# Issue-order edges between projection tiles and the state-mixing groups of a hybrid decoder block

## The chip, the cores and the metric

The kernel runs on one core of a Trainium2 chip. The metric is the device time of one execution in microseconds (us). The kernel before takes 984.88 us, the median of three runs (984.75 to 986.89). Engines are named as in the profile: PE is TensorE (matmuls, PEld its weight loads), DVE is VectorE, ACT is ScalarE, POOL is GpSimd, SP is SyncE, which issues most loads; ACTq and POOLq are the DMA issues of ACT and POOL.

## What is computed

One layer of a decoder block on 512 tokens of width 1024, all in float32. A projection of the normalised input feeds three things: r, k, v and low-rank ("lora") inputs of an RWKV-7 state recurrence over 12 heads, q, k, v of a dilated attention over 12 heads, and two gates. Cut to what matters here:

```python
h = modulate(rms_norm(x, g_pre_mix[i]), shift_m, scale_m)      # shift, scale: adaLN columns from c
p = h @ w_in[i]
pr, pk, pv, pw, pa, pg = _split(p_shift, ...)                  # token-shifted
wf = w0 + jnp.tanh(pw) @ w2                                    # lora: decay
a = jax.nn.sigmoid(a0 + pa @ a2)                               # lora: in-context rate
def step(state, inp):                                          # RWKV-7, one token
    sa = -jnp.einsum('bhvk,bhk->bhv', state, kk_t)
    state = state * w_t + sa[..., None] * (kk_t * a_t) + v_t[..., None] * k_t
    return state, jnp.einsum('bhvk,bhk->bhv', state, r_t)
y_a = (group_norm(y) + bonus) * gate @ w_a
y_b = dilated_attention_mix(pq, pk_att, pv_att, w_b)           # 3 groups of 4 heads
x = x + gate_m * rms_norm((sigmoid(ga) * y_a + sigmoid(gb) * y_b) @ w_out)
x = x + gate_f * rms_norm(swiglu(modulate(rms_norm(x))))
```

## The kernel before

**Tiles.** Every float32 matmul is done as three matmuls on split operands (`split`: `hi` a cast on ACT, L111, `lo` a subtraction on DVE, L112; `mm3`). One tile of the input projection takes 128 output columns: its 512 KB of weights are loaded, split (one `hi`, one `lo` of 128x1024), and `gemm_in` runs 8 steps of 3 matmuls of 128x512, 24 in all, into one PSUM bank. What follows depends on the kind. In the strings of `SEQ` each tile has a letter and a number: `r`, `k`, `v` are RWKV tiles (`rkv_tile`, a scale on ACT and a shift on DVE, L208), `G` gates, `Q` and `K` attention tiles (`spill_qk`: four DVE operations of rotary embedding, L227 to L236, and a store to DRAM), `V` attention values, `W` tiles of the output projection of the RWKV part. `A1` is one column of the adaLN table (a DVE multiply with accumulation, 128x1024, L168, on weights that SP loads), `N` a norm of the keys.

**Groups.** The RWKV heads are done in two groups of six heads, three pairs each (`rwkv_group(0)`, `rwkv_group(1)`; here the first and second group). For each pair PE does the lora matmuls (`lw`, `la` with `uw`, `ua`), from which ACT and DVE make decays; DVE forms `AR` and `BK` (L468 to L476); PE does the gram matmuls of AR and BK (L481, in `mm` L108), DVE masks them into `Sg` (L486), ACT copies blocks of them to `xg` (L490). PE also transposes BK (L496), computes the bonus and transposes v (L509). When all three pairs are there, DVE transposes `xg` to `fU` (L518) and inverts the triangular 32x32 blocks by 31 steps of small products and sums (L526, L530), then transposes the result to `T1` (L534). PE multiplies with it (`t1`, L547 on), and eight chunks of the recurrence follow, each a chain over PE, ACT and DVE. At the end of a group the result is normalised, transposed back (L639) and stored per pair as `d_z` (L646).

**Attention.** It reads q, k and v back from DRAM (L703 to L706) after a cosine/constant load into `cs` (L696), takes scores on PE, row maxima, exponentials on ACT (L762, L765), transposes, sums and the product with v; two of its results and the `z` of the RWKV part feed the `W` tiles.

**What sets the order.** The program is written tile by tile: `run(SEQ[0])`, group 0, `run(SEQ[1])`, group 1, `run(SEQ[2])`, attention, `run(SEQ[3])`. A scheduler places the instructions on the engines by its own estimate of when each is ready; `tc.high_priority(PRI)` around the groups and the attention lets their pieces go ahead of tiles that stand before them in the text. The result is one fixed instruction list per engine; every engine works its list in order and waits where an operand is not there.

Of the kernel before, what the change touches and what calls it, by code (L numbers as in the profile page):

```python
# [81 lines left out]


@with_exitstack
def block_kernel(ctx, tc, x, vec, cst, cst2, cst3, crow, ada, win0, lora, wts, wa, out):
# [21 lines left out]
    def mm(o, l, r, start, stop):  # L107
        return nc.tensor.matmul(o, l, r, start=start, stop=stop)  # L108

# [17 lines left out]
    def mm3(o, wh, wl, ah, al, start, stop):  # L127
        mm(o, wh, ah, start, False)
        mm(o, wh, al, False, False)
        mm(o, wl, ah, False, stop)  # L130

# [77 lines left out]

    def gemm_in(i):  # L210
        wh, wl = weights(i)
        ps = bank("mm")
        for k in range(KT):
            w = slice(k * P, (k + 1) * P)
            mm3(ps, wh[:, w], wl[:, w], hh[:, k, :], hl[:, k, :], k == 0, k == KT - 1)
        return ps
# [42 lines left out]

    def filler(i):  # L260
        ps = gemm_in(i)
        flush()
        return ps
# [110 lines left out]
    def rkv_tile(kind, pi):  # L374
        ci = {"r": 0, "k": 6, "v": 12}[kind] + pi
        ps = gemm_in(W_RK + RK_ORDER.index((kind, pi)))
        rkv[kind, pi] = tmp()[:, 0:S]
        shift_evac(ps, ci, rkv[kind, pi])
# [19 lines left out]
    def rwkv_group(gi):  # L398
# [20 lines left out]
        for p in range(GP):  # L419
            pi = p0i + p  # L420
            cols = slice(p * P, (p + 1) * P)
            sgm = rp.tile([P, 2, NCH, 2 * C], F32, tag="Sg", name=nm("Sg"), bufs=3)
            Sg[p] = sgm
            scr.append(sgm.rearrange("p e c t -> p (e c t)"))

            ps = bank(BT[gi][1])
# [8 lines left out]
            mm(ps, ua[hi64, cols], lw_l[hi64], False, True)  # L435
            A.activation(scr[p][:, 1040:1552], ps, AF.Sigmoid, bias=vcol(V_A0, pi))
        for p in range(GP):
            pi = p0i + p
# [38 lines left out]

            sgm = Sg[p]
            for c0 in (0, 4):
                pgr = [bank(BT[gi][6]), bank(BT[gi][7])]  # L480
                for c in range(c0, c0 + 4):  # L481
                    for e in range(2):
                        rows = slice(64 * e, 64 * e + 64)
                        mm(pgr[e][:, (c - c0) * P:(c - c0 + 1) * P], bk[rows, c, :], ar[rows, c, :], True, True)
                for e in range(2):
                    V.tensor_tensor(out=sgm[:, e, c0:c0 + 4, :], in0=pgr[e].rearrange("p (c t) -> p c t", c=4),  # L486
                                    in1=m_gram[:, None, :].to_broadcast([P, 4, 2 * C]), op=ALU.mult)
            for e in range(2):
                for b in range(2):
# [9 lines left out]
        for p in range(GP):  # L499
# [148 lines left out]
    def gate_tile(i):  # L648
        ps = filler(W_GATE + i)
        g = tmp("tg", 3)[:, 0:S]  # L650
# [4 lines left out]
    def run(seq):  # L655
        for item in seq.split():
# [9 lines left out]
            elif kind == "V":  # L666
                spill_v(filler(W_ATT + (n // 2) * 6 + 4 + n % 2), n // 2, d_v[n // 2][n % 2])
            elif kind == "Q":
                spill_qk(filler(W_ATT + (n // 2) * 6 + n % 2), n // 2, n % 2, d_q[n // 2][n % 2])
            elif kind == "K":  # L670
                spill_qk(filler(W_ATT + (n // 2) * 6 + 2 + n % 2), n // 2, n % 2, d_k[n // 2][n % 2])
# [387 lines left out]
```

## Time and profile before

| | before |
|---|---|
| median of three runs | 984.88 us |
| the profiled execution's own time | 985.46 us |
| its span (first to last instruction) | 983.4 us |
| PE busy | 943.3 us |
| DVE busy | 578.5 us |
| ACT busy | 394.2 us |
| POOL busy | 43.9 us |
| mean granted clock of PE | 0.982 |

The span holds all instructions; the time has 2.1 us around it. PE's busy time includes stretches at half the clock, in which the same matmuls take about twice as long, so its share of the span doesn't tell how close PE is to its best. PE's idle time and the granted clock are what an order of work can change. The other engines have time to spare over the whole span, but not in every stretch.

### The profile page before, as it was taken

What the parts mean: (1) busy time and instruction counts of PE and PEld (TensorE: products, weight loads), DVE (VectorE), ACT (ScalarE), POOL (GpSimd) and SP (SyncE); (2) the same over time, 40 slices, a digit from 0 to 9 for tenths busy, and PEclk for the clock granted to TensorE, in tenths of its full rate; (3) what the DMA queues carried; (4) which work ended last, traced back from release to release, by engine and by line L of the source; (5) the groups of instructions that cost most, each with busy time, mean ns of one, the idle gap of its engine ahead of it and who ended that gap; (6) DMA issues with size and microseconds to landing.
All of it is one profiled execution on the core that took longest, in us unless ns stands there. A gap on an engine that the chain in (4) does not pass through costs nothing.

```text
span 983.4 us, 13640 instructions
## 1 busy us (share of the span) xinstructions
PE 943.3 (96%) x5372; PEld 755.8 (77%) x5372; DVE 578.5 (59%) x1050; ACT 394.2 (40%) x631; POOL 43.9 (4%) x89
## 2 busy tenths in 40 slices
PE   6999999899989999997999899999999999999997
PEld 4886878677677776786887678988888888888885
DVE  7985789764799956685555677573333333322234
ACT  7567562433466333321472246532323222221223
POOL 0000000100100010020000100010000000000000
PEclk9998999999989999999899999999999999999999
DMA  9753215543221334249336862163242323233322
GB/s 376 276 172 102 87 54 170 174 152 106 89 70 61 110 118 150 87 166 281 99 104 226 277 224 80 44 235 107 86 129 87 107 88 105 89 104 92 101 86 85
DMA packets 47169, 131.71 MB, mean 134 GB/s; under 512 B 11249, under 2 KB 12033, under 8 KB 47106
## 3 DMA queue, kind: packets, MB, share of 16 engines
q1 hardware_dynamic: 27792, 96.74, 30.3%
q10 hardware_dynamic: 13970, 16.27, 5.3%
q0 software_dynamic: 5344, 17.84, 4.8%
q8 instruction: 42, 0.69, 0.3%
q14 instruction: 21, 0.17, 0.1%
HBM read 116.14 MB, written 14.69 MB: 133 GB/s over the span
## 4 chain that ended last, share of the span: by engine, by line
PE 71%; DVE 12%; issue 8%; DMA 4%; ACT 3%; ACTq 1%; POOL 0%; SPq 0%; DVEq 0%; POOLq 0%
PE ps L108 69%; DVE lo L112 2%; DVE fP L526 2%; DVE fT L530 2%; DMA d_ya<-t 1%; DMA k<-d_k 1%; ACT xg L490 1%; DMA x<-in_x_dram 1%; DMA gb<-d_gate 1%; ACT hi L111 1%; PE ps L308 1%; PE ps L496 0%; DVE T L534 0%; PE ps L917 0%; DMA aw<-in_ada_dram 0%
## 5 line engine op out<-in xcount | busy, mean ns | idle before, releaser
L111 ACT CAST hi<-raw 128x1024 fp32r<-128x1024 f32 (+1 forms) x130 | 132.9, 1024 | 363.2 <-PE ps L108 309.9
L112 DVE TENSOR_TENSOR lo<-raw,hi 128x1024 fp32r<-128x1024 f32 (+1 forms) x130 | 154.6, 1189 | 169.3 <-ACT hi L111 167.0
L108 PE MATMUL ps<-hl,hi 128*128 128x512 f32 x432 | 175.4, 406 | 0.0
L108 PE MATMUL ps<-hh,lo 128*128 128x512 f32 x432 | 174.7, 404 | 0.0
L108 PE MATMUL ps<-hh,hi 128*128 128x512 f32 x432 | 173.6, 411 | 0.5 <-ACT hi L111 0.5
L108 PE MATMUL ps<-h2h,hi 128*128 128x512 f32 (+1 forms) x352 | 133.6, 381 | 0.7 <-ACT u L947 0.7
L108 PE MATMUL ps<-h2l,hi 128*128 128x512 f32 (+1 forms) x352 | 133.6, 381 | 0.0
L108 PE MATMUL ps<-h2h,lo 128*128 128x512 f32 (+1 forms) x352 | 133.4, 380 | 0.0
L108 PEld LDWEIGHTS ps<-hh,hi 128*128 128x128 f32 x432 | 83.1, 193 | 19.4 <-issue 1.1
L108 PEld LDWEIGHTS ps<-hh,lo 128*128 128x128 f32 x432 | 82.9, 192 | 17.9 <-issue 0.7
L108 PEld LDWEIGHTS ps<-hl,hi 128*128 128x128 f32 x432 | 83.3, 193 | 16.6 <-issue 0.2
L108 PEld LDWEIGHTS ps<-h2h,hi 128*128 128x128 f32 x352 | 66.0, 188 | 13.5 <-ACT u L947 0.9
L108 PEld LDWEIGHTS ps<-h2l,hi 128*128 128x128 f32 x352 | 66.1, 188 | 12.8
L108 PEld LDWEIGHTS ps<-h2h,lo 128*128 128x128 f32 x352 | 66.1, 188 | 12.5
L168 DVE SCALAR_TENSOR_TENSOR aw<-aw,silur 128x1024 f32<-128x1024 f32 x48 | 58.3, 1218 | 5.8 <-DMA aw<-in_ada_dram 5.7
L948 DVE TENSOR_TENSOR u<-u,ps 128x512 f32<-128x512 f32 x22 | 15.0, 687 | 66.3 <-PE ps L108 58.7
L108 PE MATMUL ps<-lo,fh 128*128 128x512 f32 x144 | 44.4, 389 | 0.0
L108 PE MATMUL ps<-hi,fl 128*128 128x512 f32 x144 | 44.4, 389 | 0.0
L108 PE MATMUL ps<-hi,fh 128*128 128x512 f32 x144 | 44.3, 390 | 0.0
L108 PEld LDWEIGHTS ps<-lo,fh 128*128 128x128 f32 x144 | 27.0, 188 | 5.6
L108 PEld LDWEIGHTS ps<-hi,fh 128*128 128x128 f32 x144 | 27.0, 188 | 5.6
L108 PEld LDWEIGHTS ps<-hi,fl 128*128 128x128 f32 x144 | 27.0, 188 | 5.6
(294 smaller groups left out, 1365.7 us busy)
## 6 DMA issues: line engine op xcount, KB each, us to landing
raw<-in_wts_dram SPq DMA_DIRECT2D x124, 512.0 KB, 3.6
aw<-in_ada_dram SPq DMA_DIRECT2D x40, 512.0 KB, 4.4
d_gate<-t POOLq DMA_DIRECT2D x16, 256.0 KB, 2.4
aw<-in_ada_dram POOLq DMA_DIRECT2D x8, 512.0 KB, 4.7
raw<-in_win_dram SPq DMA_DIRECT2D x8, 384.0 KB, 6.6
raw<-in_wa_dram SPq DMA_DIRECT2D x8, 384.0 KB, 3.0
x<-in_x_dram SPq DMA_DIRECT2D x4, 512.0 KB, 5.0
t<-d_gate ACTq DMA_DIRECT2D x8, 256.0 KB, 4.0
```

The source lines that it names most:

```text
L108: return nc.tensor.matmul(o, l, r, start=start, stop=stop)
L111: A.copy(hi, src)
L112: V.tensor_tensor(out=lo, in0=src, in1=r32(hi), op=ALU.subtract)
L168: V.scalar_tensor_tensor(out=aw, in0=aw, scalar=1.0, in1=silur, op0=ALU.mult, op1=ALU.mult, accum_out=modv[:, i:i + 1])
L308: nc.tensor.transpose(pt[:, i * P:(i + 1) * P], xt[i][:, j * P:(j + 1) * P], ident)
L490: A.copy(xg[64 * e + 32 * b:64 * e + 32 * b + 32, :, p * NCH:(p + 1) * NCH], sgm[32 * b:32 * b + 32, e, :, 32 * b:32 * b + 32].rearrange(" ...
L526: V.tensor_tensor(out=pv, in0=fU[:, t + 1 + a:t + 1 + b, t, None].to_broadcast([P, b - a, m]), in1=fT[:, t, None, 0:m].to_broadcast([P, b ...
L530: V.tensor_tensor(out=rows, in0=rows, in1=pv, op=ALU.add)
L948: V.tensor_tensor(out=u, in0=u, in1=pg, op=ALU.mult)
```

## The change

Three things are changed; no arithmetic is.

1. `SEQ`: the third part has its attention tiles in another order (Q0, K2, K4, Q1, K1 instead of Q1, K1, K2 and Q0, K4 at the end), and the gate tile G9 moves from the head of the fourth part to the end of the third. The fourth part runs under an issue edge behind the last attention matmul of its kind (`issue_after`).
2. In `rwkv_group` the transposes of v (four for each pair, and two ACT copies to `UV`) move from behind the bonus to a loop of their own right after the lora matmuls.
3. A table `JOINTS` gives six edges. Each ties one recorded set of PE matmuls (the lora matmuls of group 0, the grams of pair 1 and 2 of group 0, the first `t1` matmuls of group 0, the grams of pair 0 of group 1, the first `t1` matmuls of group 1) to a step of a tile (`gemm_in` records the last matmul of each of its 8 steps): the set may not be placed ahead of that step. The edge is one of order alone; no semaphore is waited on for it.

```diff
@@ -77,8 +77,12 @@
-       "V5 V1 V0 V4 V2 K0 V3 Q1 K1 A1 A1 K2 A1 A1 Q3 A1 Q0 A1 Q5 A1 K4",
-       "G9 G10 G11 G12 G15 W0 G14 W1 W4 W2 W3 W5 W6 W7"]
+       "V5 V1 V0 V4 V2 K0 V3 Q0 K2 A1 A1 K4 A1 A1 Q1 A1 K1 A1 Q3 A1 Q5 G9",
+       "G10 G11 G12 G15 W0 G14 W1 W4 W2 W3 W5 W6 W7"]
+
+
+JOINTS = [("lora0", "v2", 5), ("gram01", "G4", 7), ("gram02", "k5", 7), ("inv0", "G8", 3),
+          ("gram10", "V5", 4), ("inv1", "V2", 7)]
...
     def mm(o, l, r, start, stop):
-        return nc.tensor.matmul(o, l, r, start=start, stop=stop)
+        i = nc.tensor.matmul(o, l, r, start=start, stop=stop)
+        if joint[0] is not None:
+            joined.setdefault(joint[0], []).append(i)
+        return i
+
+    joint, joined, steps = [None], {}, {}
...
+    def join():
+        for name, item, k in JOINTS:
+            if name in joined and item in steps:
+                for i in joined.pop(name):
+                    tc.add_manual_dep(ins_of(i), ins_of(steps[item][k]).name,
+                                      mybir.DependencyInfo(mybir.DependencyClass.NoSync, mybir.DependencyReason.DATA), reason="joint")
...
+        for p in range(GP):
+            v = rkv["v", p0i + p]
+
+            pt = bank(BT[gi][5])
+            for t in range(NTT):
+                nc.tensor.transpose(pt[:, t * P:(t + 1) * P], v[:, t * P:(t + 1) * P], ident)
+            ptv = pt.rearrange("p (i e w) -> p i e w", i=NTT, e=2)
+            for par in range(2):
+                A.copy(UV[64:128, par::2, :, p, :], ptv[64 * par:64 * par + 64])
...
-
-            pt = bank(BT[gi][5])
-            for t in range(NTT):
-                nc.tensor.transpose(pt[:, t * P:(t + 1) * P], v[:, t * P:(t + 1) * P], ident)
-            ptv = pt.rearrange("p (i e w) -> p i e w", i=NTT, e=2)
-            for par in range(2):
-                A.copy(UV[64:128, par::2, :, p, :], ptv[64 * par:64 * par + 64])
...
         for p in range(GP):
             pq = bank("c")
+            joint[0] = f"inv{gi}" if p == 0 else None
...
         flush()
+        join()
```

In the printed orders that follow, a number behind a name tells its buffers apart, and a line of "..." stands for rows that repeat the pattern. Line numbers of the changed kernel are larger (L108 becomes L112, L496 and L466 become L529 and L497, L112 becomes L131).

PE, around the gram matmuls of the second group's first pair (`AR`, `BK` the operands; `ps_2480` is the tile r4, `ps_2514` is v5, `ps_3498` is V5). Before:

```order
L466 MATMUL ps_2630<-cs_67,BK_2629 128x128 x4
L108 MATMUL ps_2480<-hh,hi_2476 128x512
L108 MATMUL ps_2480<-hl,hi_2476 128x512
L108 MATMUL ps_2480<-hh,lo_2477 128x512
...
L108 MATMUL ps_2645<-AR_2628,BK_2629 128x128
L108 MATMUL ps_2646<-AR_2628,BK_2629 128x128
...
L496 MATMUL ps_2673<-cs_67,BK_2629 128x128 x4
L496 MATMUL ps_2679<-cs_67,BK_2629 128x128 x4
L466 MATMUL ps_2696<-cs_67,BK_2695 128x128 x4
L108 MATMUL ps_2514<-hh,hi_2510 128x512
```

After:

```order
L529 MATMUL ps_2694<-cs_67,BK_2650 128x128 x4
...
L464 MATMUL ps_2633<-cs_67,t_2539 128x128 x4
...
L112 MATMUL ps_3498<-hh,hi_3494 128x512
L112 MATMUL ps_3498<-hl,hi_3494 128x512
L112 MATMUL ps_3498<-hh,lo_3495 128x512
...
L112 MATMUL ps_2666<-AR_2649,BK_2650 128x128
L112 MATMUL ps_2667<-AR_2649,BK_2650 128x128
...
L529 MATMUL ps_2700<-cs_67,BK_2650 128x128 x4
L497 MATMUL ps_2717<-cs_67,BK_2716 128x128 x4
```

The gram stood behind 18 matmuls of r4; it stands behind the rest of r4, all of v5 and G13 and 15 matmuls of V5 now, and a transpose of BK and those of v (L464) are ahead of it.

DVE, the end of the second group's chain to T (`fP`, `fT` the small products and sums; `lo` a weight split, `aw` an adaLN column, `t` on L247 to L252 the rotary products of a tile). Before:

```order
L526 TENSOR_TENSOR fP_2852<-fU_2850,fT_2851 128x56 x2
L530 TENSOR_TENSOR fT_2851<-fT_2851,fP_2852 128x2x28 x2
L112 TENSOR_TENSOR lo_3692<-raw_3689,hi_3691 128x1024
L526 TENSOR_TENSOR fP_2852<-fU_2850,fT_2851 128x87
L530 TENSOR_TENSOR fT_2851<-fT_2851,fP_2852 128x3x29
L526 TENSOR_TENSOR fP_2852<-fU_2850,fT_2851 128x60
L530 TENSOR_TENSOR fT_2851<-fT_2851,fP_2852 128x2x30
L526 TENSOR_TENSOR fP_2852<-fU_2850,fT_2851 128x31
L530 TENSOR_TENSOR fT_2851<-fT_2851,fP_2852 128x31
L534 STREAM_TRANSPOSE T_465_2974<-fT_2851 32x1024 x2
```

After:

```order
L556 TENSOR_TENSOR fT_2851<-fT_2851,fP_2852 128x3x29
L252 TENSOR_TENSOR t_3730<-t_3730,t_3728 128x512
L552 TENSOR_TENSOR fP_2852<-fU_2850,fT_2851 128x60
L247 STREAM_SHUFFLE t_3807<-ps_3774 128x512
L556 TENSOR_TENSOR fT_2851<-fT_2851,fP_2852 128x2x30
L249 TENSOR_TENSOR t_3809<-ps_3774,cs_143 128x512
L187 SCALAR_TENSOR_TENSOR aw_3942,modv<-aw_3942,silur 128x1024
L552 TENSOR_TENSOR fP_2852<-fU_2850,fT_2851 128x31
L131 TENSOR_TENSOR lo_3907<-raw_3904,hi_3906 128x1024
L556 TENSOR_TENSOR fT_2851<-fT_2851,fP_2852 128x31
L250 TENSOR_TENSOR t_3807<-t_3807,cs_143 128x512
L560 STREAM_TRANSPOSE T_465_2974<-fT_2851 32x1024 x2
```

One weight split stood among these last steps; now splits, an adaLN column and rotary products of two tiles stand between nearly every two of them.

PE, from the last transposes of the second group (`yb`) to the first attention scores (`k`, `q`; `ps_3992` is the tile Q5, `ps_4034` K4, `ps_4535` G10, `ps_4569` G11, `ps_4637` G15). Before:

```order
L639 MATMUL ps_3480<-cs_67,yb_3081 128x128 x4
L108 MATMUL ps_3992<-hl,hi_3988 128x512
...
L108 MATMUL ps_4034<-hh,hi_4030 128x512
...
L108 MATMUL ps_4535<-hh,hi_4531 128x512
...
L108 MATMUL ps_4126<-k_4085,q_4079 128x128
```

After:

```order
L667 MATMUL ps_3480<-cs_67,yb_3081 128x128 x4
L112 MATMUL ps_4569<-hl,hi_4565 128x512
...
L112 MATMUL ps_4603<-hh,hi_4599 128x512
...
L112 MATMUL ps_4637<-hh,hi_4633 128x512
...
L112 MATMUL ps_4160<-k_4119,q_4113 128x128
```

Between them stood 11 matmuls of Q5, K4, G9 and 9 of G10 (68 matmuls); now 11 of G11, G12 and 4 of G15 (39) stand there, and Q5, K4, G9 and G10 are ahead of the transposes.

## Rows read from the trace of the kernel before

**Rows 1.** The page's busy times of the engines, and the view of cores

```profile
PE 943.3 (96%) x5372; PEld 755.8 (77%) x5372; DVE 578.5 (59%) x1050; ACT 394.2 (40%) x631; POOL 43.9 (4%) x89
...
core 0: 983.4 us, clock 0.982
```

**Rows 2.** Waits of PE: us in total, times, longest us

```profile
PE ps L108 <- DVE BK L474: 5.2, 4, 2.9
PE ps L108 <- DVE T L534: 4.0, 3, 2.1
...
PE ps L509 <- ACT BK L497: 2.5, 2, 1.4
```

**Rows 3.** Windows: us, busy by engine (PE, PEld, DVE, ACT, POOL), clock, DMA, GB/s

```profile
91.00:98.00 7.00, 7.00 (x17) 4.71 (x16) 1.01 (x3) 3.73 (x5) 0.00 (x0) 0.53 0.22 77
279.37:285.40 6.03, 6.03 (x44) 5.81 (x45) 5.27 (x7) 3.15 (x6) 0.00 (x0) 0.51 0.39 105
427.30:522.00 94.70, 88.82 (x522) 73.48 (x520) 54.92 (x75) 38.40 (x69) 7.99 (x15) 0.95 0.54 175
487.00:505.00 18.00, 18.00 (x131) 15.71 (x129) 5.88 (x8) 17.83 (x42) 0.00 (x0) 1.00 0.08 24
```

**Rows 4.** Timeline of PE, 272 to 293: start, us, engine, line, op [idle before]

```profile
274.26 0.39 PE L108 MATMUL ps<-hh,hi 128*128 128x512 f32 x1
...
276.08 0.39 PE L108 MATMUL ps<-hh,lo 128*128 128x512 f32 x1
279.37 3.79 PE L108 MATMUL ps<-AR,BK 64*128 64x128 f32 x32 [2.90 <-DVE BK L474]
283.08 1.97 PE L496 MATMUL ps<-cs,BK 128*128 128x128 f32 x8
```

**Rows 5.** Timeline of PE: first lora matmul; second group, pair 2

```profile
76.21 0.49 PE L108 MATMUL ps<-lw_h,uw 128*128 128x512 f32 x1 [0.70 <-DVE uw L112]
...
301.89 2.06 PE L108 MATMUL ps<-AR,BK 64*128 64x128 f32 x32 [0.42 <-DVE BK L474]
...
308.61 0.66 PE L509 MATMUL ps<-cs,t 128*128 128x128 f32 x4 [1.40 <-ACT BK L497]
```

**Rows 6.** Timeline of PE, first use of T in the second group

```profile
339.17 0.28 PE L108 MATMUL ps<-T,Sg 32*32 32x32 f32 x2 [1.73 <-DVE T L534]
...
343.62 0.63 PE L108 MATMUL ps<-hh,lo 128*128 128x512 f32 x1
...
346.18 0.63 PE L108 MATMUL ps<-hh,lo 128*128 128x512 f32 x1
```

**Rows 7.** Groups of DVE, 308 to 338 us: busy us, mean ns, idle before

```profile
L530 DVE TENSOR_TENSOR fT<-fT,fP 128x110 f32<-128x110 f32 (+35 forms) x59 | 12.5, 251 | 0.1
L526 DVE TENSOR_TENSOR fP<-fU,fT 128x110 f32<-128x110 f32 (+35 forms) x59 | 12.5, 251 | 0.6
L112 DVE TENSOR_TENSOR lo<-raw,hi 128x1024 fp32r<-128x1024 f32 x4 | 4.9, 1219 | 0.0
```

**Rows 8.** Groups of DVE over the whole span, same columns

```profile
L168 DVE SCALAR_TENSOR_TENSOR aw<-aw,silur 128x1024 f32<-128x1024 f32 x48 | 58.3, 1218 | 5.8 <-DMA aw<-in_ada_dram 5.7
...
L230 DVE TENSOR_TENSOR t<-t,cs 128x512 f32<-128x512 f32 x12 | 8.2, 684 | 0.0
```

**Rows 9.** Timelines of PE, POOL and ACT, 426 to 522 us

```profile
427.26 0.60 PE L639 MATMUL ps<-cs,yb 128*128 128x128 f32 x4
430.24 0.54 POOL L646 DMA_DIRECT2D d_z<-bonus  x1 [1.38 <-DVE bonus L645]
438.98 0.33 ACTq L696 DMA_DIRECT2D cs<-in_cst_dram  x1
445.27 2.98 PE L108 MATMUL ps<-k,q 64*128 64x128 f32 x16 [1.94 <-DMA k<-d_k]
460.52 3.63 PE L108 MATMUL ps<-k,q 64*128 64x128 f32 x32 [1.32 <-DMA k<-d_k]
521.92 0.48 PE L108 MATMUL ps<-zh,lo 128*128 128x512 f32 x1
```

**Rows 10.** The page's DMA issues: KB each, median us to landing

```profile
d_gate<-t POOLq DMA_DIRECT2D x16, 256.0 KB, 2.4
```

More of the change, by code (lines that the diff above doesn't have):

```diff
@@ L107, in mm, with ins_of @@
     def mm(o, l, r, start, stop):
-        return nc.tensor.matmul(o, l, r, start=start, stop=stop)
+        i = nc.tensor.matmul(o, l, r, start=start, stop=stop)
[3 more added lines that the diff above has]
+    joint, joined, steps = [None], {}, {}
+    def ins_of(i):
+        return i.ins if hasattr(i, "ins") else i
+    def join():
[4 more added lines that the diff above has]
+                                      mybir.DependencyInfo(mybir.DependencyClass.NoSync, mybir.DependencyReason.DATA), reason="joint")
     def split(hi, lo, src):
@@ L129, in mm3 @@
         mm(o, wh, al, False, False)
-        mm(o, wl, ah, False, stop)
+        return mm(o, wl, ah, False, stop)
     vc = const.tile([P, NV], F32, name="vc")
@@ L208, in shift_evac, with gemm_in @@
         V.scalar_tensor_tensor(out=dst[:, 1:S], in0=ps[:, 0:S - 1], scalar=vcol(V_MU, ci), in1=dst[:, 1:S], op0=ALU.mult, op1=ALU.add)
-    def gemm_in(i):
+    def gemm_in(i, item=None):
         wh, wl = weights(i)
         ps = bank("mm")
+        steps[item] = []
         for k in range(KT):
             w = slice(k * P, (k + 1) * P)
-            mm3(ps, wh[:, w], wl[:, w], hh[:, k, :], hl[:, k, :], k == 0, k == KT - 1)
+            steps[item].append(mm3(ps, wh[:, w], wl[:, w], hh[:, k, :], hl[:, k, :], k == 0, k == KT - 1))
         return ps
@@ L258, in spill_v, with filler @@
         pend.append(rest)
-    def filler(i):
-        ps = gemm_in(i)
+    def filler(i, item):
+        ps = gemm_in(i, item)
         flush()
@@ L375, in rkv_tile @@
         ci = {"r": 0, "k": 6, "v": 12}[kind] + pi
-        ps = gemm_in(W_RK + RK_ORDER.index((kind, pi)))
+        ps = gemm_in(W_RK + RK_ORDER.index((kind, pi)), f"{kind}{pi}")
         rkv[kind, pi] = tmp()[:, 0:S]
@@ L424, in rwkv_group @@
             scr.append(sgm.rearrange("p e c t -> p (e c t)"))
+            joint[0] = f"lora{gi}"
             ps = bank(BT[gi][1])
@@ L435, in rwkv_group @@
             mm(ps, ua[hi64, cols], lw_l[hi64], False, True)
+            joint[0] = None
             A.activation(scr[p][:, 1040:1552], ps, AF.Sigmoid, bias=vcol(V_A0, pi))
+        for p in range(GP):
[6 more added lines that the diff above has]
+                A.copy(UV[64:128, par::2, :, p, :], ptv[64 * par:64 * par + 64])
         for p in range(GP):
@@ L478, in rwkv_group @@
             sgm = Sg[p]
+            joint[0] = f"gram{gi}{p}"
             for c0 in (0, 4):
@@ L487, in rwkv_group @@
                                     in1=m_gram[:, None, :].to_broadcast([P, 4, 2 * C]), op=ALU.mult)
+            joint[0] = None
             for e in range(2):
@@ L547, in rwkv_group @@
                     mm(pq[64 * e + 32:64 * e + 64, c * 32:(c + 1) * 32], Sg[p][0:32, e, c, 32:64], t1a[:, e, :, p * NCH + c], True, True)
+            joint[0] = None
             qs = Qd[:, p % 2]
@@ L648, in gate_tile @@
     def gate_tile(i):
-        ps = filler(W_GATE + i)
+        ps = filler(W_GATE + i, f"G{i}")
         g = tmp("tg", 3)[:, 0:S]
@@ L666, in run @@
             elif kind == "V":
-                spill_v(filler(W_ATT + (n // 2) * 6 + 4 + n % 2), n // 2, d_v[n // 2][n % 2])
+                spill_v(filler(W_ATT + (n // 2) * 6 + 4 + n % 2, item), n // 2, d_v[n // 2][n % 2])
             elif kind == "Q":
-                spill_qk(filler(W_ATT + (n // 2) * 6 + n % 2), n // 2, n % 2, d_q[n // 2][n % 2])
+                spill_qk(filler(W_ATT + (n // 2) * 6 + n % 2, item), n // 2, n % 2, d_q[n // 2][n % 2])
             elif kind == "K":
-                spill_qk(filler(W_ATT + (n // 2) * 6 + 2 + n % 2), n // 2, n % 2, d_k[n // 2][n % 2])
+                spill_qk(filler(W_ATT + (n // 2) * 6 + 2 + n % 2, item), n // 2, n % 2, d_k[n // 2][n % 2])
             elif kind == "A":
```

## The prediction

> **What bounds the kernel now.** The page comes first: TensorE (PE) is busy for 943.3 of 983.4 us, VectorE (DVE) for well under two thirds, so no other engine is the bound over the whole run, and the mean granted clock is 0.982 [rows 1]. Two things are therefore left for a change of order: the 40 us in which PE stands, and the stretches in which it runs at 1.2 instead of 2.4 GHz. A matmul of a projection tile follows the one before after 0.228 us at the full clock (274.26 to 276.08 is eight steps) [rows 4] and after 0.427 us at half (343.62 to 346.18 is six) [rows 6]; a tile of 24 thus costs 5.5 us.
>
> The list of PE's waits comes next. Those that this change can touch are the ones on BK (the last DVE product before a pair's gram matmuls, 5.2 us in four waits), on T (the inverted 32x32 blocks, 4.0 us in three) [rows 2] and on k (the attention's keys coming back from DRAM, 1.94 and 1.32 us) [rows 9]. The timeline around the largest of them shows what such a wait really costs. At 276.3 PE has run out of tiles that the program lets it do and stands 2.90 us until BK is there; the gram matmuls then take 3.79 us [rows 4], where those of another pair take 2.06 [rows 5], and the granted clock from there to 285.4 is 0.51 [rows 3]: it has dropped to half after the idle time. The same is seen behind T: the wait of 1.73 us at 339.17 is followed by matmuls at 0.427 us [rows 6]. So each wait counts with the slow matmuls behind it.
>
> **Part 1: the lora, gram and transposes pieces (edges lora0, gram01, gram02, gram10, and the value transposes).** They remove nothing; they put tiles that PE has anyway ahead of pieces that DVE has not fed yet.
> - lora0: the first lora matmul waits 0.70 us for uw [rows 5]. It now stands six matmuls later (1.4 us at 0.228), which covers it: +0.7 us (gains carry a plus). If the cast of uw is late by as much again, nothing.
> - Pairs 1 and 2 of the first head group: waits on BK there are 5.2 - 2.90 - 0.42 = 1.9 us [rows 2, 4, 5]. The grams of pairs 0, 1 and 2 now stand 18, 14 and 10 tile matmuls later; as pair 0's is later too, DVE starts each pair up to 4.1 us later on PE's account, and pairs 1 and 2 keep less of their shift than it seems. With the transposes of v no longer queued behind a PSUM copy on ScalarE (ACT), which takes up to 2.5 - 1.40 = 1.1 us more [rows 2, 5], I take +1.7 us; bounds 0 and +3.0.
> - The second group: pair 0's gram moves from behind 18 matmuls of r4 to behind 15 of V5, with v5 and G13 in between: from the lora piece on PE has 82 matmuls ahead of it instead of 26, 12.8 us more. What goes is the wait of 2.90, the 0.42 at pair 2, the 1.40 at the bonus and transposes [rows 4, 5], and the slow clock: 3.79 - 2.06 = 1.7 on the gram, and at the same ratio 0.9 of the 1.97 on the transposes. Sum 2.90 + 0.42 + 1.40 + 1.7 + 0.9 = +7.3 us. Late next would be DVE: it was 2.90 behind PE, and the tiles put in between bring it up to four weight splits of 1.22 us [rows 7] and two evacuations, 6.3 us; 12.8 - 2.9 - 6.3 leaves 3.6 us. So it fits, and the bounds are +4.5 and +8.
> - Key norm of the first group: the clock is at 0.53 from 91 to 98 us [rows 3], 3.3 us lost after small matmuls and an idle PE. Value transposes now stand in that neighbourhood and the lora wait ahead of it is gone. Between 0 and +3.3; I take +1.5, the middle, since rows speak for neither end.
>
> The Trainium skill has a rule that speaks against counting the slow clock so high: "TensorE: Matmul & The Clock Gate", Part 1, says that an idle array falls to 1.2 GHz, which the trace shows, and that the ramp costs less than 1% of a typical kernel's span, which would be under 9.8 us here. The trace disagrees: 0.982 of the clock is 1.8%, 17.7 us [rows 1]. By the page's figure the clock parts of my gains (1.7 + 0.9 + 1.5) would shrink to 9.8/17.7 of their size, an estimate of 1.8 us less in the sum; the measurement decides, and my sum goes by it.
>
> **Part 2: the T pieces (edges inv0, inv1).** The first matmul on T waits 2.1 us in the first group, 1.73 in the second [rows 2, 6]. The edges only forbid a place earlier than the third step of G8 and the seventh of V2; the scheduler now puts the pieces at the end of G8 and in K4, later than that. On DVE the chain to T is some 118 small products and sums and a transpose [rows 7], in one in-order queue; what stands in it from other work delays T one for one.
> - First group: 14 more tile matmuls ahead of T (3.2 us), three groups of value transposes (0.66 each [rows 5]) and the 1.1 us of waits less, so PE comes 0.1 us later. DVE has two adaLN columns of 1.22 us more [rows 8] in the chain, and less of splits and evacuations, net about 2.0. The wait grows to about 4: -1.8 us; bounds -4 and +2.
> - Second group: 56 more tile matmuls (12.7 us), minus 2.0 of value transposes and 1.4 of wait, plus 0.5: PE comes 9.8 us later. In the chain now stand seven weight splits instead of four, five adaLN columns instead of none and seven rotary products (tiles K0 and Q0): 3 x 1.22 + 5 x 1.22 + 7 x 0.68 [rows 7, 8] = 14.5, a little less as neighbours overlap: 14.0. The wait becomes 1.73 + 14.0 - 9.8 = 5.9 us. The slow matmuls behind it cost what they cost now. -4.0 us; bounds -6.5 (a later column whose DMA is late) and +1.7 (the wait gone). What is queued behind T on DVE is two more transposes and the recurrence's copies, which wait with it.
>
> **Part 3: the end of the second group and the attention.** Pushing 12 to 13 us of tiles ahead of T, and G9 ahead of the queue, uses up cover. Between the last transposes of the group (427.26) and the last attention matmul (521.92) lie 94.7 us now [rows 9]; in them PE has 211 matmuls of tiles, and in the changed order 100. So 111 x 0.228 = 25.2 us of work stands ahead of that stretch; the stretch has to get shorter by as much, or the difference is lost.
> It can: the cosine load that opens the attention (438.98) waits for the last rotary product of K4 now, 11.7 us after the transposes; after the change it waits for the z of the last pair, whose store is issued at 430.24 [rows 9]; stores from this queue land 2.4 us after issue [rows 10], so about 5.3 us after the transposes. From there 6.3 us to the first scores, the second wait on k, and 61.4 us from 460.52 to the end [rows 9] with 104 tile matmuls of which 49 stay (12.5 us less). What can't shrink is the run of exponentials: ACT is busy 17.83 of 18.00 us from 487 on [rows 3]. If all the 12.5 and the 4.3 us between the two waits go, the stretch is 5.3 + 6.3 + 11.0 + 48.9 = 71.5 us, a loss of 2.0. If half of the 12.5 and none of the 4.3 goes, 82 us, a loss of 12.5. I take -3.0, near the first, since most of the stretch is pieces of attention with tiles between them, which shorten one for one; and leave the other end to a rival.
>
> **The sum.** 0.7 + 1.7 + 7.3 + 1.5 - 1.8 - 4.0 - 3.0 = +2.4 us. Against the profiled execution's own 985.46 that gives 983.1; it lies 0.6 above the median of the three times (984.88), so 982.5 for the median.
>
> **Rivals.**
> - *Slower: the attention runs bare.* With 100 matmuls left, ACT's exponentials leave PE without tiles, it stands, and returns at half clock. For it: 17.83 of 18 us of ACT, two waits on k, a stage whose mean clock is 0.95 [rows 3]. Against it: the first load starts 6 us earlier. The point from which it decides: a stretch from the last transposes to the last attention matmul of more than 74.9 us eats the whole gain; at 82 us the sum is 2.4 - 9.5 = -7.1 us, at 79 us -4.1. Time 989.
> - *No change: T takes it back.* Both T waits at their bounds (-4 and -6.5) cost 4.7 us more: 2.4 - 4.7 = -2.3, with half of that 984.9 to 986. For it: the count of DVE work above is firm, since the queue is in order. Against it: nothing but DMA could make it worse than counted. Time 985.
> - *A larger gain.* The attention loses nothing, and T is there when PE comes: 2.4 + 3.0 + 1.8 + 4.0 = 11.2 at most; with two thirds of it 975. Against it: the DVE count.
> - *The edges do nothing.* The printed order excludes this for gram10 and the lora; for gram01, gram02 and inv1 the pieces stand later than the edge asks, so these edges alone may be idle. This changes who moves the pieces, not the sum.
>
> **How the numbers follow.** A difference within 0.2% (about what a measurement of this kernel can tell from no change) is 982.9 to 986.9. Forecast 0.33 (its own range 979 to 982.9), larger gain 0.10, no change 0.25, slower 0.32. Faster 0.43, same 0.25, slower 0.32. The range for 8 in 10 runs from 974.5, most of the larger gain, to 991, the bare attention at its worse end.
>
> **What would show it.** Right: no wait on BK over 1 us, the gram of the second group's first pair at 2.1 us, and PE's clock at 1.00 around it; T waits of about 4 and 6 us; a stretch of some 72 us from the last transposes to the end of the attention. Wrong: a second-group BK wait that lives on behind V5 (the DVE count in part 1 failed), T waits under 2 us (the count in part 2), or a stretch over 75 us with PE idle beside the exponentials (part 3).

## The result

The changed kernel takes 997.62 us (median of four runs, 996.81 to 1005.31) against 984.82 us of the kernel before on the same chip (983.36 to 986.89): a ratio of 1.0132, 95% interval 1.0089 to 1.0174. It is slower by 12.8 us where 2.4 us less were forecast, and lies outside the range. The rival that comes nearest is the one that it named "the attention runs bare".

The profiled execution takes 996.97 us (span 995.2). The page's busy times and the view of cores of the changed kernel answer to [rows 1]:

```profile
PE 946.8 (95%) x5372; PEld 759.8 (76%) x5372; DVE 578.2 (58%) x1050; ACT 395.2 (40%) x632; POOL 43.8 (4%) x89
...
core 0: 995.2 us, clock 0.972
```

The work is the same; PE is busy 3.5 us longer, since more of it runs at half clock (its mean clock is 0.972 instead of 0.982), and idle 8.3 us longer. Waits of PE in the changed kernel (us in total, times, longest), to be held against [rows 2]:

```profile
PE ps L112 <- DVE T L560: 4.9, 3, 3.2
...
PE ps L112 <- DMA k<-d_k: 3.2, 1, 3.2
PE ps L112 <- DVE BK L505: 3.0, 5, 1.1
PE ps L112 <- ACT zh L130: 2.6, 1, 2.6
PE ps L801 <- ACT S L791: 2.4, 1, 2.4
...
PE ps L801 <- DVE PT L806: 2.2, 1, 2.2
PE ps L112 <- DVE t L249: 2.0, 1, 2.0
```

The waits on BK have gone down from 5.2 to 3.0 us, with none over 1.1; those on T have gone up from 4.0 to 4.9. New, or longer than before, are the waits in the attention (zh, S, PT), and one on `t L249`, a rotary product that holds a PSUM bank.

To see where the time went, one number is worked out from the timelines at six places of every kernel: the start of an event, minus its start in the kernel before, minus 0.2267 us for each tile matmul (`hh`, `hl` against `hi`, `lo`) that PE has done more by then. It is the time lost or gained up to there with the moved work taken out. (The place "after the attention" is the first matmul of the third W tile.) The account is of one profiled execution of each kernel, which can lie far from the kernel's median (e10: 974.76 against 983.98), so a row is evidence only where several kernels show it. The differences from place to place, in us (plus is a loss), against the profiled execution of before:

| stage | predicted | the change |
|---|---|---|
| start to the first T piece (first group) | -3.9 + 1.8 | -2.9 |
| T piece to the second group's lora | 0 | +2.8 |
| lora to the second group's T piece | -7.3 + 4.0 | -2.0 |
| T piece to the last transposes of the group | 0 | +3.7 |
| last transposes to the W tiles after the attention | +3.0 | +12.2 |
| the rest | 0 | -2.0 |
| span | -2.4 | +11.8 |

Most of the miss stands in one row. The stretch from the last transposes to the last attention matmul, PE's timeline of the changed kernel (start, us, engine, line, operation, idle before it and what ended that); beside [rows 9]:

```profile
450.59 0.60 PE L667 MATMUL ps<-cs,yb 128*128 128x128 f32 x4
...
461.83 1.79 PE L112 MATMUL ps<-k,q 64*128 64x128 f32 x16 [1.76 <-DMA VN<-d_v]
...
473.04 4.58 PE L112 MATMUL ps<-k,q 64*128 64x128 f32 x32 [3.23 <-DMA k<-d_k]
480.26 0.50 PE L112 MATMUL ps<-zh,hi 128*128 128x512 f32 x1 [2.65 <-ACT zh L130]
...
499.97 1.94 PE L801 MATMUL ps<-cs,S 128*128 128x128 f32 x7 [2.43 <-ACT S L791]
...
521.65 0.79 PE L801 MATMUL ps<-cs,S 128*128 128x128 f32 x4 [2.17 <-DVE PT L806]
...
532.30 0.48 PE L112 MATMUL ps<-zl,hi 128*128 128x512 f32 x1
```

It is 81.7 us long, 13.0 less than before, with 25.2 us of tile work less in it (96 tile matmuls now stand ahead of it, 15 of the W tiles behind it). Windows of both kernels split its second half at the run of exponentials (us; busy and count of PE, PEld, DVE, ACT, POOL; granted clock; DMA share; GB/s). Before:

```profile
460.50:487.70 27.20, 25.50 (x145) 20.80 (x146) 17.84 (x26) 9.23 (x13) 2.15 (x4) 0.87 0.46 146
487.70:521.90 34.20, 33.26 (x233) 28.81 (x232) 16.90 (x19) 23.91 (x52) 1.62 (x3) 1.00 0.41 133
```

After:

```profile
473.04:499.50 26.46, 21.40 (x128) 16.54 (x128) 16.41 (x24) 5.38 (x8) 1.61 (x3) 0.85 0.49 161
499.50:532.30 32.80, 27.67 (x185) 24.71 (x186) 13.88 (x16) 20.68 (x49) 0.00 (x0) 0.81 0.25 86
```

The second half has 41 tile matmuls instead of 104, 14.3 us of work less, and is 59.3 instead of 61.4 us long. PE's busy time in it has fallen by 9.7 us only, and its idle time has grown from 2.6 to 10.2 us. In the part with the exponentials the clock, 1.00 before, is 0.81, and PE idles 5 us instead of 1. The attention's own matmuls pay for the clock: of four equal sets of 30 one takes 5.2 us and another 4.9, the other two 3.6 and 3.5. The first two of them, after:

```profile
504.96 5.22 PE L112 MATMUL ps<-PT,VN 128*128 128x128 f32 x30
...
512.68 3.62 PE L112 MATMUL ps<-PT,VN 128*128 128x128 f32 x30 [0.24 <-ACT PT L804]
```

### The profile page after: what moved, and what is told of

Read it like the earlier page. It is cut to its first block, busy times and chain, and to the rows that moved or that the text cites. A ratio compares the mean times of both kernels' runs of the same rounds, so it can differ in the third digit from the quotient of the medians.

```text
span 995.2 us, 13634 instructions
## 1 busy us (share of the span) xinstructions
PE 946.8 (95%) x5372; PEld 759.8 (76%) x5372; DVE 578.2 (58%) x1050; ACT 395.2 (40%) x632; POOL 43.8 (4%) x89
## 3 DMA queue, kind: packets, MB, share of 16 engines
q1 hardware_dynamic: 27792, 96.74, 30.2%
## 4 chain that ended last, share of the span: by engine, by line
PE 66%; issue 14%; DVE 11%; DMA 5%; ACT 2%; POOL 1%; SPq 0%; DVEq 0%; ACTq 0%; POOLq 0%
PE ps L112 64%; DMA aw<-in_ada_dram 2%; DVE lo L131 2%; DVE fP L552 2%; DVE fT L556 2%; DVE aw L187 1%; DMA x<-in_x_dram 1%; DMA d_ya<-t 1%; DMA gb<-d_gate 1%; DVE T L560 1%; DMA d_gate<-t 1%; PE ps L328 1%; PE ps L529 1%; ACT xg L523 0%; DVE den L829 0%
## 5 line engine op out<-in xcount | busy, mean ns | idle before, releaser
L131 DVE TENSOR_TENSOR lo<-raw,hi 128x1024 fp32r<-128x1024 f32 (+1 forms) x130 | 154.5, 1189 | 175.6 <-ACT hi L130 171.4
L112 PE MATMUL ps<-hl,hi 128*128 128x512 f32 x432 | 176.5, 409 | 0.0
L112 PE MATMUL ps<-hh,lo 128*128 128x512 f32 x432 | 174.8, 405 | 0.4 <-DVE lo L131 0.4
L112 PE MATMUL ps<-hh,hi 128*128 128x512 f32 x432 | 172.9, 410 | 2.0 <-DVE t L249 2.0
L112 PE MATMUL ps<-h2h,hi 128*128 128x512 f32 (+1 forms) x352 | 133.5, 381 | 0.7 <-ACT u L976 0.7
L112 PE MATMUL ps<-h2h,lo 128*128 128x512 f32 (+1 forms) x352 | 133.3, 380 | 0.3 <-DVE lo L131 0.3
L112 PE MATMUL ps<-h2l,hi 128*128 128x512 f32 (+1 forms) x352 | 133.4, 380 | 0.0
L112 PEld LDWEIGHTS ps<-hh,hi 128*128 128x128 f32 x432 | 83.2, 193 | 20.3 <-DVE t L249 2.2
L112 PEld LDWEIGHTS ps<-hh,lo 128*128 128x128 f32 x432 | 83.1, 192 | 18.6 <-DVE lo L131 1.1
L112 PEld LDWEIGHTS ps<-hl,hi 128*128 128x128 f32 x432 | 83.3, 193 | 17.8 <-issue 1.0
L112 PEld LDWEIGHTS ps<-h2h,hi 128*128 128x128 f32 x352 | 66.0, 188 | 13.7 <-ACT u L976 0.9
L112 PEld LDWEIGHTS ps<-h2h,lo 128*128 128x128 f32 x352 | 66.1, 188 | 13.3 <-DVE lo L131 0.7
L112 PEld LDWEIGHTS ps<-h2l,hi 128*128 128x128 f32 x352 | 66.1, 188 | 12.5
L112 PE MATMUL ps<-hi,fl 128*128 128x512 f32 x144 | 44.4, 389 | 0.0
L112 PE MATMUL ps<-hi,fh 128*128 128x512 f32 x144 | 44.3, 389 | 0.0
L112 PE MATMUL ps<-lo,fh 128*128 128x512 f32 x144 | 44.3, 389 | 0.0
L112 PEld LDWEIGHTS ps<-hi,fl 128*128 128x128 f32 x144 | 27.0, 188 | 5.6
L112 PEld LDWEIGHTS ps<-lo,fh 128*128 128x128 f32 x144 | 27.0, 188 | 5.6
L112 PEld LDWEIGHTS ps<-hi,fh 128*128 128x128 f32 x144 | 27.0, 188 | 5.6
```

The source lines that it names most:

```text
L112: i = nc.tensor.matmul(o, l, r, start=start, stop=stop)
L131: V.tensor_tensor(out=lo, in0=src, in1=r32(hi), op=ALU.subtract)
```

## Experiments

Every kernel was run beside the kernel before; its executions spread from 980 to 994 us over all of these runs (one more took 999), those of a variant run ten times by 7 to 12 us, so a ratio is worth no more than its interval. All variants compute the full result.

**e1: the tile order alone.** `JOINTS = []`, value transposes where they were.

> Only the order of the tiles in SEQ is changed (no edges, value transposes where they were). The groups keep their places: T comes after the same number of tiles, and the last transposes of the second group too; only the attention loses tiles inside itself (its last score stands 21 tile matmuls later, the exponentials have none left). Theory 'cover' (the 11.8 us are lost because the attention has fewer tiles to run beside it): slower by 2 to 5 us, all of it between the first scores and the end of the attention. Theory 'T' (the loss is the T waits and the slow clock behind them, in the groups): 984 to 986, no change.

0.9973 (0.9943 to 1.0004), median 981.15. The attention loses tiles inside itself and nothing is lost: the stretch behind the last transposes still has 179 tile matmuls in it. "Cover" in the form expected here, 2 to 5 us slower, falls.

**e2: the value transposes alone.** The new loop after the lora matmuls, old `SEQ`, no edges.

> Only the value transposes are moved ahead of the DVE chain. The grams of the first group stand 4 to 18 tile matmuls earlier on PE and T 23 earlier. Theory 'T': DVE delivers T when it did, PE comes 3 us earlier, so the first T wait grows to 4 or 5 us with a longer slow clock behind it, 986 to 988. Theory 'cover': the attention keeps its tiles, so 984 to 986.

1.0135 (1.0083 to 1.0188), 998.77: as slow as the whole change, from a part that had been costed as harmless, and outside both ranges. Most of it arises between the second group's lora piece and its T (+9.6 us in the account above, +6.0 in e6, which has the same list up to there). DVE's transposes that open and end the inversion chain show that the chain itself isn't longer (before: 308.05 to 337.23, 29.2 us; here 30.2), it starts later:

```profile
321.33 1.25 DVE L543 STREAM_TRANSPOSE fU<-xg 128x1024 f32<-128x1024 f32 x1 [1.27 <-ACT xg L522]
...
351.49 3.92 DVE L559 STREAM_TRANSPOSE T<-fT 32x1024 f32<-32x1024 f32 x2
```

From the lora piece (269.35) to the first of these it is 52.0 us, 42.7 before (265.34 to 308.05). About half of the loss is slow clock: over the 35 us from 265 on it is 0.76, against 0.90 in the kernel before.

```profile
265.00:300.00 35.00, 33.05 (x117) 24.22 (x116) 28.36 (x47) 19.98 (x32) 2.27 (x5) 0.76 0.28 96
```

**e3 and e4: the edges of one group each.** `JOINTS` cut to its first four entries (e3), to gram10 and inv1 (e4); all else as before.

> Only the four edges of the first group (lora0, gram01, gram02, inv0), everything else as before. Grams of that group 14, 10 and 6 tile matmuls later, T 12 later; the second group and the attention keep their places. The lora wait of 0.7 us and the BK waits of 1.9 us should go: 981.5 to 983.5, if the T wait stays at 2.1 us; if it grows by 1 to 2 us with the slow clock behind it, 983.5 to 985. Theory 'cover' says nothing can be lost here.

> Only the two edges of the second group (gram10, inv1). The gram of its first pair stands 63 tile matmuls later, T 97 later, its end 69 later, so the attention has 110 tile matmuls left instead of 179 (83 in the full change). The BK wait of 2.9 us and the slow clock behind it go, +7. Theory 'cover': at 12.2 us for 96 tiles, 69 tiles cost 8.8 us, T 1 to 4: 987 to 991. Theory 'T': the loss sits between the lora piece and the end of the recurrence, the attention itself keeps its excess over its own work: 984 to 988 with a T wait over 3 us.

e3: 1.0033 (0.9998 to 1.0067), above both expected ranges. In its profiled execution, which is 5.5 us faster than its median, what is gained up to the first T piece (3.1 us) is given back between it and the next lora piece (2.9 us; the T wait of 2.6 us stands there, behind the first two matmuls of the piece). e4: 1.0057 (1.0020 to 1.0093). The total comes near the range of "cover", the place does not: the attention, with 110 tile matmuls, loses 3.4 us where 8.8 were priced, and another 3.5 us are lost behind it. No T wait is over 2.3 us, so "T" falls. The wait of 2.9 us on BK does not go either: it stands at the transposes of BK instead of the gram (more on this below). PE's stretch from the last transposes to the last attention matmul is 81.3 us:

```profile
444.65:525.98 81.33, 73.06 (x447) 59.68 (x445) 41.87 (x56) 31.57 (x62) 5.17 (x10) 0.94 0.54 172
```

**e5 and e6: the change without its value transposes, and without its edges.**

> The whole change but for the value transposes, which stay behind the bonus. Theory 'value transposes' (new, from e2: three transposes and six ACT copies ahead of the chain make the way from the lora piece to T longer): faster than the changed kernel by 3 to 10 us, 988 to 994, with T on time. Theory 'cover': the attention has 85 tile matmuls behind the last transposes, two more than the changed kernel's 83, so it loses its 12 us all the same: 993 to 998.

> The new tile order and the value transposes without any edge. The groups stand where e2 has them, the attention keeps 174 tile matmuls as in e1. If the parts simply add: e2 (+14) and e1 (-3) give 995 to 997. Theory 'cover' says that the attention loses nothing here and gives 985 to 989. If the edges are what cures the value transposes' damage, this is slower than the changed kernel: 997 to 1002.

e5: 1.0109 (1.0058 to 1.0161), with 12.8 us lost in the attention: the value transposes are not what makes the whole change slow. e6: 1.0018 (0.9990 to 1.0047), better than the sum of e1 and e2 and next to the range of "cover": the parts do not add. Its attention loses nothing.

**e7: the gate loads of the W tiles on POOL's queue.**

```diff
-        nc.scalar.dma_start(ga, d_gate[ct])
+        G.dma_start(ga, d_gate[ct])
```

In the changed kernel two such loads stand on ACT's queue ahead of the exponentials, until a tile buffer that a gate's store still reads is free (ACT's timeline):

```profile
492.52 5.67 ACTq L841 DMA_DIRECT2D t<-d_gate  x2
498.22 1.28 ACT L791 ACT_TABLE_LOAD   x1 [5.71 <-DMA d_gate<-t]
499.52 1.60 ACT L791 ACTIVATE S<-S,negM 128x128 f32<-128x128 f32 x4
```

> The changed kernel with one edit: the loads of the gates for the W tiles are issued by POOL instead of ACT. PE and DVE keep their lists to the row. In the trace of the changed kernel such a load stands 5.7 us on ACT's queue, until a gate tile is stored, with all exponentials behind it. Theory 'queue' (half of the attention's loss is this one wait): 991 to 994, and the exponentials start 4 to 6 us earlier after the scores. Theory 'cover': the exponentials start earlier, and the same idle time moves behind them: 996 to 998.

1.0106 (1.0039 to 1.0172), between the two expected ranges. PE and DVE work the same lists. The wait is gone and another stands in its place:

```profile
487.61 1.28 ACT L791 ACT_TABLE_LOAD   x1 [0.27 <-issue]
492.44 1.60 ACT L791 ACTIVATE S<-S,negM 128x128 f32<-128x128 f32 x4 [3.55 <-DVE negM L781]
```

From `Mn` (the last DVE product ahead of it, 494.67 and 489.30 on PE) to the first exponential it was 4.85 us and is 3.14: 1.7 us of the 5.7 were real, the rest was covered by the chain of the row maxima, which ends with 2.9 us of small PE matmuls on `Mn` (at a clock of 1.00) and a DVE step. The attention still loses 11.1 us.

**e9: the gate tile G9 back at the head of the fourth part**, in the changed kernel.

```diff
-       "... Q3 A1 Q5 G9",
-       "G10 G11 ...
+       "... Q3 A1 Q5",
+       "G9 G10 G11 ...
```

> The changed kernel with the gate tile G9 back at the head of the fourth part. Up to T PE has the same list; the second group ends 27 tile matmuls (6.1 us) earlier and the attention has 110 tile matmuls behind the last transposes instead of 83. Theory 'floor' (the stretch from the last transposes to the W tiles behind the attention can't get shorter than some 83 to 86 us, however few tiles are in it: 85.8 with 83 tiles, 83.1 with 110 in e4): that stretch stays at 83 to 86 and the 6.1 us are gained, 990 to 993 beside 984 to 988 of before. Rival 'T and recurrence' (the tiles are missed in the recurrence instead): the recurrence gets longer by as much, 995 to 998.

1.0084 (1.0050 to 1.0119), 993.15. To the third W tile the stretch is 83.7 us, inside the 83 to 86 that "floor" gave; the attention's loss falls from 12.2 to 4.0 us. To the last attention matmul:

```profile
444.16:526.17 82.01, 72.86 (x446) 59.33 (x445) 41.86 (x56) 31.35 (x62) 5.17 (x10) 0.94 0.53 170
```

Over all kernels, this stretch (from the start of the last of those transposes to that of the last attention matmul) against the tile matmuls that stand in it, without and with those of the W tiles:

| tile matmuls left | with W tiles | us, last transposes to last attention matmul (kernel) |
|---|---|---|
| 83 to 85 | 100 to 102 | 81.4 (change), 80.3 (e7), 82.3 (e5) |
| 110 | 139 | 81.3 (e4), 82.0 (e9) |
| 150 to 152 | 172 to 185 | 86.1 (e11), 86.5 (e12), 87.3 (e13) |
| 179 | 201 | 87.9 (e10), 91.2 (e1) |
| 174 to 179 | 206 to 214 | 93.6 (e14), 93.8 (e15), 94.0 (e8), 94.2 (e6), 94.3 (before), 94.8 (e3), 96.1 (e2) |

From 110 matmuls to 83 (139 to 100 with the W tiles, 8.8 us of work) it doesn't get shorter. No kernel got under 80 us. Tiles taken out below 110 are missed one for one, and some of those between 150 and 110. That the 80 to 82 us are the attention's own chain alone is not shown. Of the 81 to 82 us PE stands idle for 8.3 (e4) and 9.2 (e9), but for 15.2 in the change, and the clock is 0.94 in the first two and 0.87 in the change:

```profile
450.60:532.30 81.70, 66.52 (x410) 54.91 (x409) 41.36 (x56) 29.48 (x60) 4.68 (x9) 0.87 0.49 163
```

So the missing tiles left PE idle, and the matmuls that remained ran slower. How long the stretch would be with 83 tile matmuls at the full clock, no run tells.

**e8, e10, e12, e14, e15: smaller sets.** All have the new tile order and the old place of the value transposes. e8 and e15 (the same kernel) have lora0, gram01, gram02 and gram10 at an earlier step:

```diff
+JOINTS = [("lora0", "v2", 5), ("gram01", "G4", 7), ("gram02", "k5", 7), ("gram10", "v5", 2)]
```

e10 leaves out gram10, e14 leaves out all but gram10, e12 puts it at ("v5", 5).

> A candidate: the new tile order, old value transposes, the three edges lora0, gram01 and gram02, and gram10 at the third step of v5 instead of V5, which puts the second group's first gram 9 tile matmuls later (2.0 of the 2.9 us wait) and T 9 later. The attention keeps 177 tile matmuls. Theory 'cover' and theory 'T' both: no loss at either place, 977 to 981. If a later gram alone costs what it gains, 981, as the tile order alone.

> The new tile order with lora0, gram01 and gram02 and old value transposes: e8 without gram10. It tells how much of e8 comes from the second group's first gram. Theory 'gram10 is worth its wait': the BK wait of 2.9 us and the slow clock behind it are back, 980 to 983, 4 to 7 us over e8. If the first group's edges carry the gain, 976 to 978.

> e8 with gram10 three steps later (at the sixth step of v5): the second group's first gram 9 tile matmuls later than in e8, T 10 later, the attention with 150 tile matmuls. The rest of the 2.9 us BK wait is covered: 974 to 976, if the attention still has enough tiles; theory 'cover' in its plain form (0.13 us for each tile taken) says 978 to 979.

> The new tile order and one edge, gram10 at the third step of v5. If e8's gain is this edge's: 976 to 979 (before at 985). If it needs the first group's edges: 981 to 983, as the tile order alone.

> e8 once more, word for word, with more rounds, because its neighbours e10 and e12 lay 8 us above it on another chip's runs. If e8's ratio of 0.99 is the kernel's own: 975 to 978 beside 985 of before. If it is the spread between executions: 980 to 983, the same as e10 and e12.

Ratios: e8 0.9897 (0.9844 to 0.9950), e15 0.9924 (0.9898 to 0.9951); e10 0.9967 (0.9935 to 0.9998), e12 0.9979 (0.9944 to 1.0013), e14 0.9955 (0.9920 to 0.9990), and e1 0.9973. The kernel of e8 and e15 beats the kernel before by about 8 us (976.83 against 985.50, twelve runs). It had been expected to do so by covering the BK wait of the second group, and doesn't. Waits of PE in e15:

```profile
PE ps L519 <- DVE BK L495: 2.8, 1, 2.8
...
PE ps L111 <- DVE BK L495: 1.3, 3, 0.5
```

The edge ties the gram matmuls; the transposes of the same BK (L519) are not tied, the scheduler has put them ahead of the tiles, and they now wait for what the gram waited for. The same wait of 2.8 to 2.9 us stands at these transposes in all kernels with gram10 and the old place of the value transposes (e4, e5, e8, e12, e14, e15). e12 lies above both of its expected ranges, e14 between its two, e10 near the range for a gram10 that is worth its wait. Which of the edges is worth how much these runs don't tell: the intervals of e1, e10, e12, e14 and e15 overlap.

**e11 and e13: the value transposes with the first group's edges.** e11 is e8 with the value transposes moved; e13 has them with lora0, gram01 and gram02 and the old tile order.

> e8 with the value transposes moved as in the change. The order puts the second group's first gram 14 tile matmuls later than e8, T 18 later, and leaves the attention 152 tile matmuls instead of 177. Theory 'floor': 152 tiles (34.5 us) still keep the stretch above its floor, no loss there. Theory 'value transposes' (they lengthen the chain from lora to T by 5 us or more): T waits over 3 us, 979 to 985. If the edges make them harmless: 975 to 978.

> The value transposes with lora0, gram01 and gram02, in the old tile order. In e2 the moved transposes let the scheduler bunch the second group's last two grams behind each other (behind 803, 809 and 813 tile matmuls); here these stand behind 791, 816 and 839 again, though no edge ties them. Theory 'bunching' (e2's loss is the chain to T, lengthened because the last two pairs come at once and the tiles that should cover it wait for their splits): the loss of about 8 us ahead of the second T is gone, 984 to 988 in all. Rival 'ACT copies' (the copies of v ahead of the chain cost it): the loss stays, 994 to 998.

e11: 0.9972 (0.9940 to 1.0004). Its total lies in the range of "value transposes", but not for that reason: from the lora piece to T it gains 2.0 us, and its attention loses 0.2, as "floor" had it; its profiled execution loses 6.0 us between the first T piece and the second lora piece. e13: 0.9954 (0.9930 to 0.9979), 980.55, where e2 without the edges has 998.77. The loss ahead of the second T is gone (-2.0 instead of +9.6), and from the lora piece (265.76) to the start of the chain it is 44.3 us:

```profile
310.03 1.25 DVE L543 STREAM_TRANSPOSE fU<-xg 128x1024 f32<-128x1024 f32 x1 [1.16 <-ACT xg L522]
```

The six ACT copies of v stand ahead of the chain in both, so the copies aren't the cause: "ACT copies" falls. What differs is where the scheduler puts the second group's grams among the tiles. The last two pairs are mixed with each other in e2; in e13 the first two are partly mixed and the last stands by itself. That fits "bunching", but other tiles' splits moved too, and so did the clock: over the same 35 us in which e2 had 0.76, e13 has 1.00 (e6, with the lists of e2 up to there, has 0.90 and loses 6.0 us). Slow clock is thus a large part of the late chain, and the step from the order of the grams to it is not shown.

```profile
265.00:300.00 35.00, 34.37 (x192) 26.71 (x192) 32.09 (x51) 29.98 (x46) 1.63 (x4) 1.00 0.36 111
```

## Why the prediction was wrong

**Part 3, the attention, is the step that failed.** Its first half came as worked out: the opening load is issued 5.4 us after the last transposes (5.3), the first scores stand 11.2 us after them (11.6), the second wait on k ends at 22.4 (22.6). The failed step is the next one: of 61.4 us behind the second wait 12.5 us of tiles would go, "which shorten one for one". They don't: 14.3 us of tiles went, and 61.4 became 59.3. PE's idle time there grew by 7.5 us, and its other matmuls took some 4.6 us more. Most of the tiles had stood beside the chain, not in it. The prediction had this in its other bound, 12.5 us of loss; the measured 12.2 lies there. The reason given for the near end, that tiles stand between pieces of the attention, says nothing of which of the two is waiting, and [rows 3] had evidence against it for 18 of the 61.4 us: ACT was busy for 17.83 of them, and tiles taken from PE could not shorten that. Part of what keeps the stretch long is the slow clock that the rival named: 0.81 with the exponentials, where [rows 3] had 1.00.

e4 and e9 test this by size. Both leave 110 matmuls, and lose 3.4 and 4.0 us there; e5 and e7, with 85 and 83, lose 12.8 and 11.1. The break-even of 74.9 us lay below the 80 us that no kernel got under.

Three slips in the working did not decide it. Of the 111 tile matmuls that leave the stretch 96 stand ahead of it and 15 behind it. Behind the second wait 41 of 104 are left, not 49. And two thirds of the "larger gain" of 11.2 us give 977 us, not 975.

**Part 2, the T waits.** The count of DVE work held: the second group's chain from `fU` to `T` takes 42.2 us (319.61 to 361.82) instead of 29.2, 13.0 more where 14.0 were counted. PE's wait was put at 5.9; it is 1.32 at T and 1.98 a tile earlier, on a PSUM bank that a rotary product in the same DVE queue holds. (A T wait under 2 us was to be the sign that the count had failed; the chain's length shows that it had not.) PE's timeline:

```profile
352.43 0.50 PE L112 MATMUL ps<-hh,hi 128*128 128x512 f32 x1 [1.98 <-DVE t L249]
...
363.80 0.28 PE L112 MATMUL ps<-T,Sg 32*32 32x32 f32 x2 [1.32 <-DVE T L560]
```

In the first group the wait is 3.22 us (4 predicted). What was wrong is "the slow matmuls behind it cost what they cost now". The prediction wrote this of the second group and had no term for them in the first: behind the first group's wait seven tile matmuls ran at half clock before, and fifteen do now. The window behind it has a clock of 0.56 for 11 us:

```profile
177.80:188.80 11.00, 10.96 (x56) 8.39 (x57) 7.83 (x8) 1.26 (x3) 2.89 (x4) 0.56 0.45 145
```

The second row of the table goes with these matmuls: it is -1.1 to -1.2 where none was slow (e1, e8, e10, e14), about 0 with six or seven (e4, e12, e15), +2.8 with fifteen (the change, e9, e13). It doesn't go with the length of the wait. e11 and e13 have the same lists of PE, DVE and ACT up to the second T; the first wait is 3.13 us in e11 and leaves a clock of 0.84, and 2.48 us in e13 and leaves 0.55 (each from the T piece on):

```profile
178.31:189.31 11.00, 11.00 (x67) 8.75 (x68) 9.08 (x10) 3.24 (x5) 2.91 (x4) 0.84 0.43 155
```

```profile
176.80:187.80 11.00, 11.00 (x56) 8.44 (x57) 7.82 (x8) 1.24 (x3) 2.89 (x4) 0.55 0.44 139
```

e7, with the lists of the change, has a wait of 2.44 us, four slow matmuls and +1.4. So the +2.8 is slow clock, and how much of it belongs to the change and how much to the execution is open.

**Part 1, the grams.** Right in its number for the kernel as changed: the gram of the second group's first pair takes 2.06 us, with no wait and the clock at 1.00 around it. The 0.42 us at pair 2 did not go, as was forecast: 0.76 and 1.06 us on BK stand at pairs 1 and 2. Together with part 2, lora to T is 2.0 us better, 3.3 were forecast. The lora wait is gone, and the clock at the first group's key norm (91 to 98 us) is 1.00 instead of 0.53.

The cause that it gave for the largest gain, the 56 tile matmuls that the edge gram10 puts ahead of the gram, does not hold. e5 has this edge with the value transposes in their old place, and the wait of 2.9 us is there:

```profile
PE ps L520 <- DVE BK L496: 2.9, 1, 2.9
...
PE ps L112 <- DVE BK L496: 2.6, 4, 1.1
```

e13 has the value transposes and no gram10, and no wait on BK over 0.4 us; from lora to T it gains the same 2.0 us, and its attention keeps 152 tile matmuls. (e2 and e6, without any edge, don't have this wait either, but PE waits there for a weight split, 1.8 and 2.9 us.) e10 has the edges of e13 without the value transposes, and a wait of 2.9 us. So the wait goes with the second part of the change, the value transposes, behind which the gram stands 23 tile matmuls later without an edge of its own (791 instead of 768). The edge is what takes the tiles from the attention, and it was not needed for this: here the number was right by luck. The value transposes were costed only for what they move out of the way. That they change the places of other pieces (e2) was no term at all.

**The recurrence (+3.7 us)** had no term either, and it isn't settled that it needs one. The windows of the same stretch in the changed kernel and, with PE's and DVE's lists the same to the row, in e7:

```profile
363.80:397.00 33.20, 31.01 (x259) 23.36 (x259) 21.72 (x36) 8.97 (x17) 4.99 (x8) 0.69 0.32 106
```

```profile
363.70:397.00 33.30, 31.09 (x321) 23.64 (x321) 26.67 (x47) 11.93 (x24) 4.99 (x8) 0.95 0.36 119
```

One execution got a clock of 0.69 and finished 259 matmul records, the other 0.95 and 321; from T to the last transposes they are 6.1 us apart (+3.7 and -2.4). e7's edit lies behind this stretch, and PE's waits in it are the same but for 0.2 us, so this is the spread between executions, and a loss of this size in one profile is no evidence.

**The rivals.** "The edges do nothing" stays open for inv1: no run has gram10 in the place of the change without it. "T takes it back" did not come by its waits, 3.2 and 1.3 us, both shorter than forecast; +2.8 us came behind the first of them, as slow clock. The chances had 0.32 on slower, with 989; the price was too low because the floor was taken as a bound and not as the likely case.

**The uncertainty** of 0.2% was too narrow. The kernel before spreads over 980 to 994 us, and ten runs give intervals of 0.3 to 0.4% to each side.

## What to carry to other kernels

Before work is moved out of a stretch, ask what the stretch would take with none of it: follow its own chain (loads, row maxima, exponentials, sums) from end to end, and count every tile below that length as a loss. Independent work is worth most where the chain waits longest; here 3 us of wait were to be covered with tiles that the attention then missed. An order edge moves what it is tied to and, through the scheduler, things that it is not tied to; where two kinds of instruction read the same operand (gram and transposes of BK), an edge on one hands the wait to the other.

## What the hardware showed

Behind waits of 1.7 to 3.2 us PE's tile matmuls followed each other after 0.427 us (1.2 GHz) for a while, and the length of the wait did not tell for how many: none in e10 (2.08 us), seven before (2.11), fifteen in e13 (2.48), seven in e11 (3.13), fifteen in the change (3.22). And the clock differs from execution to execution of the same lists after nearly the same waits: 0.69 and 0.95 over 33 us in the change and in e7.
